# Hybrid SSD/S5 encoder block on one core: the down projection's quarter differences move to VectorE over three products, the SSD running sums' halves take another buffer, the group norm's sums are kept by step

## The chip, the core and the metric

One NeuronCore of a Trainium2 chip runs the whole kernel: TensorE (PE) multiplies, VectorE (DVE), ScalarE (ACT) and GpSimd (POOL) do everything else, SyncE (SP) issues most transfers, POOL and ACT a few. The metric is the device time of one execution in microseconds, the median of three runs; a profiled execution has its own time.

## What is computed

One layer of a residual encoder over 1024 tokens of width 1024, in float32:

```
h    = RMSNorm(x)
p    = h @ W_in                          # z | xBC | dt | u
y_A  = SSD (Mamba-2 chunked scan, both directions), gated by silu(z), RMS-normed in 2 groups of 512
y_B  = S5 scan, gelu, GLU
x    = x + RMSNorm(concat(y_A, y_B) @ W_out)
x    = x + RMSNorm((silu(h2 @ W_gate) * (h2 @ W_up)) @ W_down),   h2 = RMSNorm(x)
```

Two parts are touched by the change. In the SSD group the decays are exponentials of running sums over a chunk of 128 tokens, and the group norm divides by the root of the mean of y*y over the 512 channels of a group. The down projection is a product of 1024x2816 by 2816x1024.

## The kernel before

All matrix products are made from float32 split in a high half of reduced precision ("fp32r") and a low half, the rest; three matmuls (high by high, high by low, low by high) stand for one. A split is always the same pair: ScalarE copies the source to the high half, VectorE subtracts that from the source.

**The SSD stretch** (about 540 to 945 us). A scheduler, by priorities and a cost table of its own, merges two generators: the GLU of the S5 group (`glu`, matmuls recorded on L277, tiles `gh`, `glo`), then the output projection (`out_s5`, `out_g0`, matmuls L1169), and the eight SSD units (`unit(q)`, q = 0 to 7, each a pair of heads). `dt_prep` comes ahead of unit 0: it makes the running sums with `tri_le`/`tri_ge`, splits them into a tile `rhl` (high half by ScalarE on L890, low half by VectorE on L891), and writes these with eight transfers on POOL's queue to two DRAM tensors, `rr_d` (L894) and `na_d` (L895). `unit_loads` reads them back as `la` and `ra`, the two operands of the matmuls on L1013 whose exponentials are the decays. `rhl` sits in the buffer with the tag "X", of which there is one; unit 0's own `X` (tokens by channels, transposes on L903, copied by ScalarE on L904) has the same tag. From `X` come `Xw` (one half by VectorE, one by POOL, L975) and from that the chunk states (matmuls L988). At its end a unit squares y (L1064 or L1067), adds that to `ssum` (L1068), splits y into `hl` (L1072, L1073; tag "hl") and stores it on SP's queue (L1074, L1075). y lies token by token, token = 8k + l; `hl` is stored by step l, so L1072 reads y with a step of eight elements. `group_norm` sums `ssum` over channels with eight matmuls by a column of ones (L1082), whose stationary operand is a slice of `ssum` with a step of eight.

**The down projection** (about 1431 to 1668 us). It runs in the order of the program, as two levels of a seven-product scheme: the quarters of the activation (computed before, stored in `ff_d`) and of W_down are combined, and seven products P1, P2, P3, P6, P5, P7, P4, each over eleven slices q, give the four quarters of the result. One (product, slice) is twelve matmuls of 128x128 by 128x512 on L1898. `d_op(i)` prepares it: loads (`wd_load`, `da`), the two splits (ScalarE L1879, VectorE L1880), then `wd_sums`, which overwrites quarters of the weight tile `wd[q]` with differences that later products use. It runs five products ahead of the matmuls (`dla`); sixteen buffers with the tag "w8" hold the eleven `wd` tiles and five `dop` tiles, so at most four prepared products wait behind the one that runs. `DB` says which quarter a product uses: P3 the raw quarter 3, P6 the changed quarter 3, P5 quarter 0, P7 quarter 1, P4 quarter 2. `half_sum` squares a finished half row block on ScalarE and multiplies it by the norm's weight (L1933); `final` adds the residual (L1951).

Of the kernel before, what the change touches and what calls it, by code (L numbers as in the profile page):

```python
# [10 lines left out]
F32R = mybir.dt.float32r  # L11
I32 = mybir.dt.int32
AF = mybir.ActivationFunctionType
ALU = mybir.AluOpType
PSUM = bass.MemoryType.PSUM
ADD, SUB, MUL = ALU.add, ALU.subtract, ALU.mult
# [116 lines left out]
def hymba_block(ctx, tc, P, out, dbg=None, upto=99):  # L133
    nc = tc.nc

    @contextmanager
    def hpri(n):
        off = KN[n]
        if off:
            p = tc.cur_priority  # L140
            tc.cur_priority = p - off
        yield
        if off:
            tc.cur_priority = tc.cur_priority + off

    def pri(n):
        def deco(f):
            def g(*a, **k):
                with hpri(n):
                    return f(*a, **k)  # L150
            return g
        return deco

    act, dve, pool, pe, sp = nc.scalar, nc.vector, nc.gpsimd, nc.tensor, nc.sync
# [5 lines left out]
    def pd(k):  # L160
        return pool if k in KN['pd'] else dve
# [39 lines left out]
    def ptmp():  # L201
        return psB.tile([128, 512], F32, tag="tmp", name="ptmp")
# [112 lines left out]
    def rms_scale(ssum, rstd, inv_n, eps):  # L315
        dve.tensor_scalar(rstd, ssum, inv_n, eps, op0=MUL, op1=ADD)
        return pool.tensor_tensor(rstd, rstd, mhalf.to_broadcast(list(rstd.shape)), op=ALU.pow)
# [246 lines left out]
    HF = [slice(0, 512), slice(512, 1024)]  # L564
# [264 lines left out]
    def dt_prep():  # L829
# [54 lines left out]
        for d in range(2):  # L884
            pe.matmul(t[:, 128 * d:128 * d + 128], af[:, d].rearrange("p c h -> p (c h)"), (tri_le, tri_ge)[d], start=True, stop=True)
            pe.transpose(t[:, 256 + 128 * d:384 + 128 * d], ln[:, d].rearrange("p c h -> p (c h)"), ident)
        rhl = un.tile([128, 2, 4, 128], F32R, tag="X", name="rhl")
        rh, rl = rhl[:, 0], rhl[:, 1]
        tv = t.rearrange("p (n l) -> p n l", n=4)
        act.copy(rh, tv)  # L890
        dve.tensor_tensor(rl, tv, rh.bitcast(F32), op=SUB)  # L891
# [71 lines left out]
    def unit(q, ssum):  # L963
        g = q // 4
        with hpri("u1"):
# [4 lines left out]
            X = un.tile([128, 8, 128], F32, tag="X", name="X")  # L970
            transposes(X, xT)
            Xw = un.tile([128, 2, 8, 2, 64], F32, tag="Xw", name="Xw")
            for d in range(2):
                w = wdt[:, :, 16 * d + 2 * q:16 * d + 2 * q + 2].unsqueeze(3).to_broadcast([128, 8, 2, 64])
# [4 lines left out]
        with hpri("u2"):  # L979

            Sn = un.tile([128, 2, 7, 128], F32, tag="Sn", name="Sn")
            for s0 in range(0, 7, 2):
                t = ptmp()
                ns = min(2, 7 - s0)
                for d in range(2):
                    for s in range(ns):
                        c = s0 + s if d == 0 else 7 - s0 - s
                        pe.matmul(t[:, 256 * s + 128 * d:256 * s + 128 * d + 128], Bt[:, c, g, :],  # L988
                                  Xw[:, d, c].rearrange("p h e -> p (h e)"), start=True, stop=True)
                for s in range(ns):  # L990
# [4 lines left out]
                    for d in range(2):  # L995
                        for hh in range(2):
                            es = slice(64 * hh, 64 * hh + 64)
                            o = 256 * s + 128 * d + 64 * hh
# [4 lines left out]
        y = un.tile([128, 1024], F32, tag="yg", name="yg", bufs=2)  # L1003
        for hf in range(2):
# [21 lines left out]
            with hpri("u4"):  # L1026
# [10 lines left out]
                for j in range(4):  # L1037
                    c = 4 * hf + j
# [4 lines left out]
                for d in range(2):  # L1043
# [7 lines left out]
                    for j in range(j0, j1):  # L1051
                        c = 4 * hf + j
# [7 lines left out]
            if hf == 0:  # L1060
                yield
        with hpri("u4"):
            if q % 4 == 0:
                act.activation(ssum, y, AF.Square)  # L1064
            else:
                sq = io.tile([128, 1024], F32, tag="io", name="sq")
                act.activation(sq, y, AF.Square)  # L1067
                pd('ss').tensor_tensor(ssum, ssum, sq, op=ADD)  # L1068
            hl = un.tile([128, 2, 8, 128], F32R, tag="hl", name="hl")
            w = vec2[:, R_N + q:R_N + q + 1]  # L1070
            yv = y.rearrange("p (k l) -> p l k", l=8)
            act.activation(hl[:, 0], yv, AF.Copy, scale=w)  # L1072
            dve.scalar_tensor_tensor(hl[:, 1], yv, w, hl.bitcast(F32)[:, 0], op0=MUL, op1=SUB)  # L1073
            Q[KN["cq"]].dma_start(ch_d[128 * q:128 * q + 128], hl.bitcast(F32)[:, 0])  # L1074
            Q[KN["cq"]].dma_start(cl_d[128 * q:128 * q + 128], hl.bitcast(F32)[:, 1])  # L1075

    @pri("gn")
    def group_norm(g, ssum):
        t = ptmp()
        sv = ssum.rearrange("p (k l) -> p l k", l=8)  # L1080
        for l in range(8):
            pe.matmul(t[:, l:l + 1], sv[:, l, :], ones[:, 0:1], start=True, stop=True)  # L1082
        rms_scale(t[:, 0:8], rg[:, g, :], 1.0 / 512, 1e-5)
# [254 lines left out]
    with tc.manual_schedule():  # L1338
        next(cvs)
        pair_powers()  # L1340
        for n, blk in enumerate(blocks):
# [9 lines left out]
            b = n - NB + KC  # L1351
# [94 lines left out]
    un = ust.enter_context(tc.tile_pool(name="un", bufs=1))  # L1446
# [8 lines left out]
    def ssd():  # L1455
        for g in range(2):
            ssum = un.tile([128, 1024], F32, tag="ssum", name="ssum")
            for q in range(4 * g, 4 * g + 4):
                yield from unit(q, ssum)
                yield  # L1460
            group_norm(g, ssum)
            yield
# [16 lines left out]
    fill = glu()  # L1479
    next(fill)  # L1480
    dt_prep()
    fill_with(fill, 15, R_GLU)
    for _ in fill:
# [278 lines left out]
    for l in range(8):  # L1762
        b = MX["step"] * l
# [11 lines left out]
        for q in range(2):  # L1775
            at(b + MX["ev"] + 0.6 * q, turn_evac, l, q)
            if l < 4 or q:
                n = "12"[q] + "12"[l // 4]
# [44 lines left out]
    for i in range(14, len(prods)):  # L1823
        p, n, m = prods[i]
# [23 lines left out]
    def wd_load(n, q):  # L1848
        if n == "P1":
            wd.append(fp.tile([128, 4, 512], F32, tag="w8", name="wd", bufs=W_))  # L1850
            bl = ((0, 0, 0),)
        elif n == "P2":
            bl = ((2, 1, 0),)
        elif n == "P3":
            bl = ((3, 1, 1), (1, 0, 1))
        else:
            return
        for b, s_, c in bl:
            sp.dma_start(wd[q][:, b], wdv[s_, c][:, q])

    def wd_sums(n, q):
        w = wd[q]
        l = {"P3": ((0, 1, 0), (1, 3, 1), (3, 3, 0), (2, 2, 3))}.get(n, ())
        for o, a, b in l:
            pool.tensor_tensor(w[:, o], w[:, a], w[:, b], op=SUB)  # L1865

    def d_op(i):
        if i >= len(dprods) or i in dops:
            return
        n, q = dprods[i]  # L1870
        wd_load(n, q)
        if (n, q // 2) not in das:
            das[n, q // 2] = a = wst.tile([128, 2, 512], F32, tag=("whi", "wlo", "raw")[len(das) % 3], name="da", bufs=2)
            e = min(2, NP - q)
            sp.dma_start(a[:, 0:e], ff_d[int(n[1]) - 1, q:q + e].rearrange("q p k -> p q k"))
        a = das[n, q // 2][:, q % 2]
        dops[i] = t = fp.tile([128, 2, 2, 512], F32R, tag="w8", name="dop", bufs=W_)
        for k, src in enumerate((a, wd[q][:, DB[n]])):
            act.copy(t[:, k, 0], src)  # L1879
            dve.tensor_tensor(t[:, k, 1], src, t.bitcast(F32)[:, k, 0], op=SUB)  # L1880
        wd_sums(n, q)
# [5 lines left out]
    wp2 = fp.tile([128, 1024], F32, name="wp2")  # L1887
# [12 lines left out]
    def d_post(n, j, ps):  # L1900
        if n == "P1":
            act.copy(us[j], ps)
        elif n == "P2":
            dve.tensor_tensor(C11[j], us[j], ps, op=ADD)
            later.append((half_sum, j, 0))
        elif n == "P3":
            act.copy(C12[j], ps)
        elif n == "P6":
            dve.tensor_tensor(us[j], us[j], ps, op=ADD)
        elif n == "P5":  # L1910
            dve.tensor_tensor(ts_[j], us[j], ps, op=ADD)
            dve.tensor_tensor(C12[j], C12[j], ts_[j], op=ADD)
            later.append((half_sum, j, 1))
            if j == 3:
                later.extend([(final_load, 0), (final_load, 1), (final_scale, 0), (final, 0), (final_scale, 1), (final, 1), (final_store, 0), (final_load, 2), (final_store, 1), (final_load, 3),
                              (final_scale, 2), (final, 2), (final_scale, 3), (final, 3), (final_store, 2), (final_store, 3)])
        elif n == "P7":
            dve.tensor_tensor(C22[j], ts_[j], ps, op=ADD)
            dve.tensor_tensor(us[j], us[j], ps, op=ADD)
            later.append((half_sum, 4 + j, 1))  # L1920
            later.append((final_load, 4 + j))
        else:
            dve.tensor_tensor(C21[j], us[j], ps, op=ADD)
            half_sum(4 + j, 0)
            final(4 + j)

    def half_sum(l, c):
        f = fa[:, l, HF[c]]
        act.activation(jk2, f, AF.Square, accum_out=s5[:, c, l:l + 1])
        last = (l, c) in ((4, 0), (5, 0), (6, 0), (7, 0))  # L1930
        if last:
            final_scale(l)
        (dve if last else pool).tensor_tensor(f, f, wp2[:, HF[c]], op=MUL)  # L1933

    def final_scale(l):
        dve.tensor_tensor(s5[:, 2, l:l + 1], s5[:, 0, l:l + 1], s5[:, 1, l:l + 1], op=ADD)
        rms_scale(s5[:, 2, l:l + 1], s5[:, 3, l:l + 1], 1.0 / 1024, 1e-6)
# [73 lines left out]
```

## Time and profile before

| | us |
|---|---|
| median of 3 runs (lowest, highest) | 1672.16 (1668.52, 1672.4) |
| the profiled execution, its own time | 1669.68 |
| its span from first to last instruction | 1667.8 |
| PE busy in the span | 1546.0 (93%) |
| DVE busy | 1241.3 (74%) |
| ACT busy | 730.4 (44%) |
| POOL busy | 461.4 (28%) |

Starts of rows are microseconds from the span's start. The profiled execution's time is 1.9 us over its span and 2.5 us under the median. Busy shares are averages over stages with different limits; what an edit is worth is read from its own stage.

### The profile page before, as it was taken

To read this page: it belongs to the slowest core of one execution; us is meant where nothing else is said; L and a number is where in the kernel's file an instruction comes from. 1 tells how busy PE (TensorE), PEld (TensorE's weight loads), DVE (VectorE), ACT (ScalarE), POOL (GpSimd) and SP (SyncE) were. 2 spreads that over 40 slices of the span, in tenths; PEclk is the share of its full clock that TensorE was granted. 3 is DMA by queue.
4 is the path that set the end of the run, shared out by engine and by line. 5 is a ranking of instruction groups with operands and counts; after the bars stand their busy time and mean duration, and the time that the engine had idled before them with its cause. 6 is when DMAs were issued, how large, how long until landed. Compare 5 with 4: busy or idle time off the path is not lost.

```text
span 1667.8 us, 22199 instructions
## 1 busy us (share of the span) xinstructions
PE 1546.0 (93%) x7980; PEld 1263.7 (76%) x7980; DVE 1241.3 (74%) x1910; ACT 730.4 (44%) x1238; POOL 461.4 (28%) x455
## 2 busy tenths in 40 slices
PE   7999999999777889899999988999999999999897
PEld 6787788777775667778778766788888888787686
DVE  7549998888452687886666578788878887669777
ACT  6345632323887445444343476222223322344352
POOL 2110000000221120111110141555555544249412
PEclk9999999999898989999999998999999999999999
DMA  5553444433877657976588872332222221682234
GB/s 181 149 144 103 127 159 152 133 109 105 207 173 204 189 176 245 289 227 219 189 262 269 291 237 95 122 107 96 95 101 101 95 101 51 242 313 74 92 119 170
DMA packets 250000, 271.58 MB, mean 163 GB/s; under 512 B 29387, under 2 KB 190659, under 8 KB 249891
## 3 DMA queue, kind: packets, MB, share of 16 engines
q1 hardware_dynamic: 224515, 215.96, 41.6%
q0 software_dynamic: 12896, 33.83, 6.4%
q10 hardware_dynamic: 12480, 20.39, 3.4%
q8 instruction: 63, 1.03, 0.3%
q14 instruction: 46, 0.38, 0.1%
HBM read 185.23 MB, written 84.84 MB: 162 GB/s over the span
## 4 chain that ended last, share of the span: by engine, by line
PE 40%; DVE 10%; DMA 8%; issue 4%; ACT 4%; POOL 3%; SPq 0%; DVEq 0%; POOLq 0%; ACTq 0%
PE acc L1592 13%; PE ptmp L1592 10%; PE ptmp L1898 4%; PE acc L1169 3%; PE acc L1898 3%; DVE dop L1880 2%; PE acc L277 2%; DMA m<-m_d 2%; PE ptmp L988 1%; POOL wd L1865 1%; PE ptmp L1054 1%; DMA m_d<-m 1%; DMA oraw<-in_w_out_dram 1%; DVE cacc L756 1%; PE ptmp L1040 1%
## 5 line engine op out<-in xcount | busy, mean ns | idle before, releaser
L1169 PE MATMUL acc<-ohi,cat 128*128 128x512 f32 x512 | 173.3, 404 | 10.8 <-DMA cat<-ch_d 5.7
L277 PE MATMUL acc<-hTh,whi 128*128 128x512 f32 (+1 forms) x456 | 179.5, 394 | 0.4 <-ACT hTh L334 0.4
L277 PE MATMUL acc<-hTl,whi 128*128 128x512 f32 (+1 forms) x456 | 178.7, 392 | 0.5 <-DVE hTl L337 0.5
L277 PE MATMUL acc<-hTh,wlo 128*128 128x512 f32 (+1 forms) x456 | 178.0, 391 | 0.0
L1575 DVE TENSOR_TENSOR wop<-rawp,wop 128x512 fp32r<-128x512 f32 x120 | 137.7, 1148 | 17.9 <-ACT wop L1574 16.7
L1592 PE MATMUL ptmp<-T,wop 128*128 128x512 f32 x528 | 127.8, 398 | 4.1 <-ACT T L1748 3.7
L1592 PE MATMUL acc<-T,wop 128*128 128x512 f32 x528 | 125.7, 393 | 1.7 <-DVE T L1751 1.6
L1898 PE MATMUL ptmp<-dop 128*128 128x512 f32 x528 | 122.0, 392 | 2.9 <-DVE dop L1880 2.9
L1592 PE MATMUL acc<-B,wop 128*128 128x512 f32 x528 | 124.6, 391 | 0.0
L1169 PEld LDWEIGHTS acc<-ohi,cat 128*128 128x128 f32 x512 | 97.7, 192 | 34.4 <-DVE mix L1720 5.4
L1592 PEld LDWEIGHTS ptmp<-T,wop 128*128 128x128 f32 x528 | 101.0, 192 | 27.3 <-ACT T L1748 3.9
L1898 PEld LDWEIGHTS ptmp<-dop 128*128 128x128 f32 x528 | 100.1, 190 | 24.2 <-DVE dop L1880 3.2
L1592 PEld LDWEIGHTS acc<-T,wop 128*128 128x128 f32 x528 | 98.8, 188 | 25.1 <-DVE T L1751 3.4
L1592 PEld LDWEIGHTS acc<-B,wop 128*128 128x128 f32 x528 | 99.0, 188 | 21.9 <-DVE B L1751 0.3
L1607 ACT ACTIVATE cg<-cg 128x512 f32<-128x512 f32 x44 | 27.8, 633 | 183.0 <-DVE cg L1605 183.0
L1574 ACT CAST wop<-rawp 128x512 fp32r<-128x512 f32 x120 | 70.2, 615 | 76.7 <-POOL rawp L1549 51.2
L1880 DVE TENSOR_TENSOR dop<-da,dop 128x512 fp32r<-128x512 f32 x77 | 75.1, 975 | 37.5 <-ACT dop L1879 37.4
L1898 PE MATMUL acc<-dop 128*128 128x512 f32 x396 | 95.6, 398 | 7.4 <-DVE dop L1880 4.7
L1169 PE MATMUL acc<-olo,cat 128*128 128x512 f32 x256 | 101.9, 398 | 0.4 <-DVE olo L1133 0.4
L277 PEld LDWEIGHTS acc<-hTh,whi 128*128 128x128 f32 x456 | 86.7, 190 | 19.4 <-issue 1.7
L277 PEld LDWEIGHTS acc<-hTl,whi 128*128 128x128 f32 x456 | 86.7, 190 | 18.4 <-DVE hTl L337 1.0
L277 PEld LDWEIGHTS acc<-hTh,wlo 128*128 128x128 f32 x456 | 86.7, 190 | 17.1 <-DVE wlo L268 0.2
(368 smaller groups left out, 3400.5 us busy)
## 6 DMA issues: line engine op xcount, KB each, us to landing
ff_d<-cg POOLq DMA_DIRECT2D x77, 256.0 KB, 2.3
da<-ff_d SPq DMA_DIRECT2D x35, 512.0 KB
raw<-in_w_in_dram SPq DMA_DIRECT2D x28, 512.0 KB
cat<-ch_d SPq DMA_DIRECT2D x48, 256.0 KB
cat<-cl_d SPq DMA_DIRECT2D x48, 256.0 KB
wd<-in_w_down_dram SPq DMA_DIRECT2D x44, 256.0 KB
rawp<-in_w_gate_dram SPq DMA_DIRECT2D x10, 1024.0 KB
rawp<-in_w_up_dram SPq DMA_DIRECT2D x10, 1024.0 KB
```

What stands on the lines that cost most here:

```text
L277: pe.matmul(ps, a[:, k, :], b[:, k, sl], start=(k == 0 and n == 0), stop=(k == 7 and n == 2))
L756: (pool if ct in KN['pc'] and k in KN['pk'] else dve).scalar_tensor_tensor(a[:, d], xp[:, r], w[k], a[:, d], op0=MUL, op1=ADD)
L988: pe.matmul(t[:, 256 * s + 128 * d:256 * s + 128 * d + 128], Bt[:, c, g, :], Xw[:, d, c].rearrange("p h e -> p (h e)"), start=True, stop=True)
L1040: pe.matmul(yd[64 * hh:64 * hh + 64, 128 * j:128 * j + 128], X[:, c, 64 * hh:64 * hh + 64], Ms[hh][:, j, :], start=True, stop=True)
L1054: pe.matmul(yo[:, 128 * j:128 * j + 128], Sn[:, d, st, :], CT[:, g, 128 * c:128 * c + 128], start=True, stop=True)
L1169: pe.matmul(ps, c[:, a, k % 4, :], b[:, k % 2, :], start=(k == 0 and n == 0), stop=(k == n_ - 1 and n == 2))
L1574: act.copy(t[:, 0], src)
L1575: dve.tensor_tensor(t[:, 1], src, t.bitcast(F32)[:, 0], op=SUB)
L1592: pe.matmul(ps, a[:, ai, k, :], b[:, bi, k, :], start=(k == 0 and q == 0), stop=(k == 3 and q == 2))
L1607: act.activation(cg[:, 0], cg[:, 0], AF.Silu)
L1880: dve.tensor_tensor(t[:, k, 1], src, t.bitcast(F32)[:, k, 0], op=SUB)
L1898: pe.matmul(ps, t[:, 0, a, 128 * j:128 * j + 128], t[:, 1, b, :], start=(q == 0 and n == 0), stop=(q == NP - 1 and n == 2))
```

## The change

Four edits. `rhl` takes the tag "hl" in place of "X" (it fills half of that tile). The squares of y are written by step: L1064 and L1067 now read y with a step of eight and write in order, and `group_norm` reads `ssum` in order. In the down projection quarter 1 of the weights is loaded with P2 in place of P3; of the four differences one is made with P2, two with P3 and one with P6, where all four were made with P3, and they go from POOL to VectorE. The multiplications by the norm's weight that POOL made go to VectorE too.

```diff
-        rhl = un.tile([128, 2, 4, 128], F32R, tag="X", name="rhl")
-        rh, rl = rhl[:, 0], rhl[:, 1]
+        rhl = un.tile([128, 2, 8, 128], F32R, tag="hl", name="rhl")
+        rh, rl = rhl[:, 0, 0:4], rhl[:, 1, 0:4]
...
+            yv = y.rearrange("p (k l) -> p l k", l=8)
             if q % 4 == 0:
-                act.activation(ssum, y, AF.Square)
+                act.activation(ssum.rearrange("p (l k) -> p l k", l=8), yv, AF.Square)
             else:
                 sq = io.tile([128, 1024], F32, tag="io", name="sq")
-                act.activation(sq, y, AF.Square)
+                act.activation(sq.rearrange("p (l k) -> p l k", l=8), yv, AF.Square)
                 pd('ss').tensor_tensor(ssum, ssum, sq, op=ADD)
...
-        sv = ssum.rearrange("p (k l) -> p l k", l=8)
+        sv = ssum.rearrange("p (l k) -> p l k", l=8)
...
         elif n == "P2":
-            bl = ((2, 1, 0),)
+            bl = ((2, 1, 0), (1, 0, 1))
         elif n == "P3":
-            bl = ((3, 1, 1), (1, 0, 1))
+            bl = ((3, 1, 1),)
...
-        l = {"P3": ((0, 1, 0), (1, 3, 1), (3, 3, 0), (2, 2, 3))}.get(n, ())
+        l = {"P2": ((0, 1, 0),), "P3": ((1, 3, 1), (3, 3, 0)), "P6": ((2, 2, 3),)}.get(n, ())
         for o, a, b in l:
-            pool.tensor_tensor(w[:, o], w[:, a], w[:, b], op=SUB)
+            dve.tensor_tensor(w[:, o], w[:, a], w[:, b], op=SUB)
...
-        (dve if last else pool).tensor_tensor(f, f, wp2[:, HF[c]], op=MUL)
+        dve.tensor_tensor(f, f, wp2[:, HF[c]], op=MUL)
```

The order in the down projection is the program's. Here is VectorE around the end of P2, before: the pairs of splits, and P2's four sums (L1904).

```order
L1880 TENSOR_TENSOR dop<-da,dop 128x512
L1880 TENSOR_TENSOR dop<-wd,dop 128x512
L1904 TENSOR_TENSOR fa<-fa,acc 128x512 x4
L1880 TENSOR_TENSOR dop<-da,dop 128x512
L1880 TENSOR_TENSOR dop<-wd,dop 128x512
```

And the same place after (lines from 1064 on have moved by one):

```order
L1881 TENSOR_TENSOR dop<-da,dop 128x512
L1881 TENSOR_TENSOR dop<-wd,dop 128x512
L1866 TENSOR_TENSOR wd<-wd 128x512 x2
L1905 TENSOR_TENSOR fa<-fa,acc 128x512 x4
L1881 TENSOR_TENSOR dop<-da,dop 128x512
L1881 TENSOR_TENSOR dop<-wd,dop 128x512
L1866 TENSOR_TENSOR wd<-wd 128x512 x2
L1934 TENSOR_TENSOR fa<-fa,wp_11882 128x512
```

Each pair of splits of P3 is now followed by two differences (L1866), and the first four also by a multiplication (L1934).

In the SSD stretch the scheduler places the rows anew, on every engine from the running sums of `dt_prep` on; PE's order is the old one again from the last blocks of the GLU on. On POOL, at the writes of `rhl`, the difference is:

```order
 L940 MEMSET efs 128x256
 L894 DMA rr_d<-rhl 8x16x128
+L975 TENSOR_TENSOR Xw<-X,wdt 128x1024
 L895 DMA na_d<-rhl 2x64x128
 L894 DMA rr_d<-rhl 8x16x128
@@ -99,5 +100,4 @@
 L894 DMA rr_d<-rhl 8x16x128
 L895 DMA na_d<-rhl 2x64x128
-L975 TENSOR_TENSOR Xw<-X,wdt 128x1024
 L1034 TENSOR_TENSOR M<-E 128x512
```

Unit 0's `Xw` on POOL stood behind all eight writes and now stands behind the first, so seven writes are issued after it. On PE, before, 44 matmuls of the GLU stand between the last transpose of `dt_prep` (L886) and unit 0's chunk states (L988), one between these and the decays' matmuls (L1013, L1014):

```order
L277 MATMUL acc<-gh,whi 128x512
L277 MATMUL acc<-glo,whi 128x512
L988 MATMUL ptmp<-Xw,Bt 128x128 x14
L277 MATMUL acc<-gh,wlo 128x512
L1013 MATMUL ptmp<-ra_4786,la_4785 128x512
L1014 MATMUL ptmp<-neg,idr 128x512
```

After, 18 stand ahead of the chunk states and 22 between these and the decays' matmuls (four of the 44 have gone ahead of the transposes); here is the first of the two places:

```order
L277 MATMUL acc<-gh,wlo 128x512
L277 MATMUL acc<-gh,whi 128x512
L988 MATMUL ptmp<-Xw,Bt 128x128 x14
L277 MATMUL acc<-glo,whi 128x512
L277 MATMUL acc<-gh,wlo 128x512
```

Some two dozen matmuls of the GLU have moved from ahead of the chunk states to behind them.

## Rows read from the trace of the kernel before

**Rows 1.** Busy time by stretch: window, us, PE, PEld, DVE, ACT, POOL, PEclk, DMA share, GB/s

```profile
1431.00:1490.00 59.00, 56.11 (x242) 46.38 (x242) 36.04 (x49) 27.29 (x51) 10.99 (x11) 0.97 0.94 345
1490.00:1530.00 40.00, 39.38 (x173) 31.98 (x172) 39.67 (x28) 21.40 (x42) 38.67 (x24) 1.00 0.28 89
1530.00:1566.00 36.00, 29.19 (x111) 20.62 (x110) 31.00 (x23) 9.49 (x18) 31.98 (x21) 0.96 0.20 67
```

**Rows 2.** PE in order of time, blocks P3, P6 and P5: start, us

```profile
1495.06 30.08 PE L1898 MATMUL ptmp<-dop 128*128 128x512 f32 x132
1524.97 0.39 PE L1898 MATMUL acc<-dop 128*128 128x512 f32 x1
...
1567.64 30.11 PE L1898 MATMUL ptmp<-dop 128*128 128x512 f32 x132
```

**Rows 3.** POOL in order of time, its differences in the down projection

```profile
1486.47 36.82 POOL L1865 TENSOR_TENSOR wd<-wd 128x512 f32<-128x512 f32 x22 [11.49 <-DVE dop L1880]
...
1550.43 12.57 POOL L1865 TENSOR_TENSOR wd<-wd 128x512 f32<-128x512 f32 x8
```

**Rows 4.** DVE in order of time, splits beside POOL and after POOL has ended

```profile
1508.47 1.78 DVE L1880 TENSOR_TENSOR dop<-da,dop 128x512 fp32r<-128x512 f32 x1
...
1564.07 0.68 DVE L1880 TENSOR_TENSOR dop<-wd,dop 128x512 fp32r<-128x512 f32 x1
1564.67 0.68 DVE L1880 TENSOR_TENSOR dop<-da,dop 128x512 fp32r<-128x512 f32 x1
```

**Rows 5.** ACT in order of time, a split of P6; idle time before it in brackets

```profile
1547.10 0.62 ACT L1879 CAST dop<-wd 128x512 fp32r<-128x512 f32 x1 [7.35 <-POOL wd L1865]
```

**Rows 6.** A group from 1220 us on: count, busy us, mean ns, idle before

```profile
L1865 POOL TENSOR_TENSOR wd<-wd 128x512 f32<-128x512 f32 x44 | 70.5, 1606 | 49.4 <-DMA wd<-in_w_down_dram 35.4 <-DVE dop L1880 11.5
```

**Rows 7.** The chain of waits in the tail: start, us, what

```profile
1641.14 3.40 DVE fa L1951 x2
...
1645.00 5.43 DMA xr<-x_d
...
1650.52 1.42 DVE fa L1951 x2
```

**Rows 8.** POOL in order of time, in the tail

```profile
1640.92 6.03 POOL L1933 TENSOR_TENSOR fa<-fa,wp 128x512 f32<-128x512 f32 x4
```

**Rows 9.** PE in order of time, unit 0's chunk states

```profile
587.08 1.19 PE L988 MATMUL ptmp<-Xw,Bt 128*128 128x128 f32 x4 [9.14 <-DVE Xw L975]
588.75 5.37 PE L988 MATMUL ptmp<-Xw,Bt 128*128 128x128 f32 x24 [0.48 <-POOL Xw L975]
```

**Rows 10.** The chain of waits, the last write of rhl and Xw

```profile
575.56 8.97 DMA na_d<-rhl
...
585.75 2.95 POOL Xw L975
```

**Rows 11.** Busy time by stretch, columns as in rows 1, unit 0's chunk states

```profile
587.00:594.00 7.00, 6.44 (x29) 6.17 (x30) 6.43 (x17) 2.14 (x4) 1.70 (x1) 0.51 0.41 116
```

**Rows 12.** ACT's groups of 128x1024 from 128x1024, columns as in rows 6

```profile
L1072 ACT ACTIVATE hl<-yg,vec 128x1024 fp32r<-128x1024 f32 x8 | 18.4, 2303 | 0.0
...
L1729 ACT ACTIVATE xn<-xr,s 128x1024 f32<-128x1024 f32 x8 | 9.2, 1152 | 6.5 <-POOL s L1716 6.5
...
L1067 ACT ACTIVATE sq<-yg 128x1024 f32<-128x1024 f32 x6 | 6.4, 1059 | 22.3 <-DVE yg L1059 22.3
```

**Rows 13.** The chain of waits at the ends of units 2 and 7

```profile
724.99 1.06 ACT sq L1067
...
914.50 2.38 ACT hl L1072
...
919.55 4.28 DMA m<-m_d
```

**Rows 14.** PE in order of time, group 0's norm sums and a stretch of chunk states

```profile
764.05 3.26 PE L1082 MATMUL ptmp<-ones,ssum 128*128 128x1 f32 x14
...
680.80 1.83 PE L988 MATMUL ptmp<-Xw,Bt 128*128 128x128 f32 x14 [0.99 <-POOL Xw L975]
```

More of the change, by code (lines that the diff above doesn't have):

```diff
@@ L1070, in unit @@
             w = vec2[:, R_N + q:R_N + q + 1]
-            yv = y.rearrange("p (k l) -> p l k", l=8)
             act.activation(hl[:, 0], yv, AF.Copy, scale=w)
```

## The prediction

> **What bounds the kernel now.** Over the span TensorE is the busy engine, so the question is where it waits. I read the table of busy time by stretch first. In the down projection PE fills the stretch to 1530, but VectorE and POOL fill it too, 39.67 and 38.67 of 40 us; in the next 36 us PE is busy for 29.19 only, while the DMA queues lie at a share of 0.20 [rows 1]. So it is an engine that holds PE there, no transfer.
>
> PE's own timeline shows how much that is. Product P3 takes from 1495.06 to 1524.97, that is 29.91 us for 132 matmuls, without a wait. P6, the same 132 matmuls, takes from 1524.97 to 1567.64, that is 42.67 [rows 2]. **The loss is 42.67 - 29.91 = 12.76 us**, and no other product has one of its kind.
>
> The cause is read on three engines. POOL makes the weight differences without a break from 1486.47 to 1563.0 [rows 3], 44 of them at 1606 ns [rows 6], with the multiplications between. While it does, a split on VectorE takes 1.78 us; as soon as POOL is through, the same instruction takes 0.68 and the next one starts 0.60 later [rows 4]. Two splits at 1.7 us apart are 3.4 us a product where PE needs 29.91 / 11 = 2.72, so VectorE falls behind through P3 and eats the four prepared products. In P6 ScalarE waits as well, 7.35 us at once, for a quarter that POOL has not made yet [rows 5]. Both waits have one source: POOL does this work at 1.6 us an instruction and makes VectorE slow meanwhile.
>
> **The change part by part.**
>
> *Differences and multiplications to VectorE.* POOL loses all 44 differences and its 12 multiplications (16 halves less the last four); it keeps only the small power of the norm. With POOL idle I take 0.68 us for each of these on VectorE, at a spacing of 0.60 [rows 4]: same shape, same two operands in SBUF. (From above: 1.78, if something else than POOL should make these slow; then see the rivals.) A product of P2 or P6 needs two splits and one difference, 3 x 0.60 = 1.8 us of PE's 2.72. P3 needs two splits and two differences, 4 x 0.60 = 2.4 a product, 26.4 for eleven, and beside that P2's four sums and four multiplications, 8 x 0.60 = 4.8: together 31.2 us against PE's 29.91. VectorE falls back by 1.3 us; with single durations of 0.68 instead of the spacing (52 x 0.68 = 35.4) by 5.5 us. The cover is the four prepared products, 4 x 2.72 = 10.9 us, which are full when P3 begins, as P2 leaves VectorE a third of its time. So PE should not wait in P3 or P6. P6's quarter 3 is then made with P3, eleven products ahead of its use. **Term: -12.7 us** (bounds: 0 and -12.8).
>
> *Quarter 1 with P2.* Eleven loads of 256 KB come eleven products earlier. In the stretch where they fall the DMA engines move 345 GB/s at a share of 0.94 [rows 1]; P2's product then needs 3 x 0.262 MB (two quarters of weights, one of activations) in 2.72 us, 289 GB/s, and P3's needs 193 where it needed 289. Less than the rate shown, so hidden behind P1 and P2's matmuls. Were the cover gone, 11 x 0.262 MB at 345 GB/s would be 8.4 us. I take 0.
>
> *The tail.* With P4's matmuls four multiplications on POOL (6.03 us in all [rows 8]) run beside the last residual of the first four row blocks, which takes 3.40 us for two instructions; undisturbed, two such take 1.42 [rows 7]. The store of that block and the loads of the last four `xr` are queued behind it on SP: they start at 1645.00 and land at 1650.4, and the final work of block 4 on VectorE waits for that [rows 7]. With POOL idle the loads start 3.40 - 1.42 = 2.0 us earlier. Against that VectorE now makes the four multiplications itself, 4 x 0.60 = 2.4 us, directly behind that residual, in a place where it would wait for the loads anyway. What follows per block is serial on VectorE and goes along. **Term: -1.8 us** (0 to -2.0).
>
> *`rhl` in another buffer.* Now unit 0's X waits for the last write of `rhl`, which lands at 575.56 + 8.97 = 584.53 [rows 10], and PE waits 9.14 us for the `Xw` made of it [rows 9]. After, X is copied at once. But two things give most of that back. First, on POOL's queue `Xw` (2.95 us [rows 10]) now stands behind the first write, so the other seven are issued later by that, and ScalarE makes the two copies of X ahead of the running sums: the last write lands near 588. Second, `la` and `ra` are read back from these writes, and the decays' matmuls need them: a load on SP's queue lands some 4 us after its issue (4.28 in [rows 13]), so they can start near 592. Before, they started one matmul behind the chunk states, whose rows end at 588.75 + 5.37 = 594.1 [rows 9]. So the wait moves from the chunk states to the decays and PE gains about 2 us of its 9.14. The clock takes part of it: behind the wait the granted clock was 0.51, the lower of the two levels (1.2 GHz against 2.4), and 24 matmuls took 5.37 us, 0.224 each [rows 9, 11], where elsewhere 14 take 1.83, 0.131 each [rows 14]. With a wait ahead of the decays, their ten larger matmuls pay instead. **Term: -1.2 us** (+1 to -9.1, the whole wait).
>
> *Squares by step.* Eight squares on ScalarE, 1059 ns each now. What they will cost is shown by a neighbour: the same engine's copy of the same y with the step of eight takes 2303 ns, while a copy with a scale that reads in order takes 1152 [rows 12]. I take 2.3 us, 1.25 more each, 10.0 for eight (bounds: 0 and 10). Of that counts what lies on the path: unit 2's square and unit 7's stand in the chain of waits, and behind unit 7's the split and then the load of `m` on SP's queue [rows 13]; of the other six I count one. **Term: +3.7 us.**
>
> The Trainium skill speaks against this edit ("SBUF — State Buffer", section "Door 1: The DMA port swizzle"): SBUF is read in lines of 16 bytes, and each access that passes to a new line pays. A step of eight float32 passes to a new line with every element. By it all eight squares become slow, and the sum would be the same as by the row of the copy; the column sums below would become faster, for the same reason.
>
> *`ssum` read in order.* Fourteen loads and matmuls by the column of ones took 3.26 us, 0.233 each [rows 14]; a stationary operand of the same size read in order gives 0.131 a matmul [rows 14]. Sixteen for a group are 1.6 us, of which group 0's lie in a stretch that PE fills; group 1's lie ahead of a wait for `m` and gain nothing. **Term: -1.4 us.**
>
> **Sum:** -12.7 - 1.8 - 1.2 + 3.7 - 1.4 = -13.4 us on an execution of 1669.68, that is 1656.3. The median shown lies 2.5 us above that execution, the lowest run 1.2 below; I give 1657.
>
> **The rivals.**
>
> *A. VectorE becomes the bound.* In P3 it has 52 instructions (44 + 8). PE waits as soon as they take more than 29.91 + 10.9 = 40.8 us, 0.785 each; the whole gain of P6 is used up at (40.8 + 12.8) / 52 = 1.03 us each, and at 1.7, today's spacing, the down projection would be about 35 us slower, some 1692. For it: 1.7 us is what rows of this very stretch show. Against it: the splits fall back to 0.68 in the moment POOL ends [rows 4], with the same operands, and POOL has nothing left to do.
>
> *B. The SSD stretch eats the gain.* All eight slow squares lie on the path (+10.0) and the decays wait as long as the chunk states did (no gain from `rhl`): -12.7 - 1.8 + 10.0 = -4.5, 1665. For it: the units' work feeds loads on SP's in-order queue. Against it: between the first and the last unit PE is the engine that ends most pieces of the chain.
>
> *C. The wait for `rhl` goes entirely*, and PE's clock with it: -9.1 in place of -1.2, 1648 to 1649. Against it: the decays still need data that leave later.
>
> *D. The loads with P2 come late:* up to 8.4 us of the gain, 1665. Against it: the rate above.
>
> **How the numbers follow.** Forecast, P6's wait gone and the SSD stretch within a few us either way: 0.66, its own range 1652 to 1662. C 0.13, B 0.10, D 0.04, A with a gain left 0.02 and A slower 0.05. What a measurement of this kernel can tell from no change is 0.3%, 5 us. Forecast, C, and the better halves of B, D and A are faster by more: 0.87; within 0.3%: 0.08; slower: 0.05. The range reaches to C's 1648 and to B's and D's 1666.
>
> **What would show it.** Right: PE without waits from P1's second product to P4's end, each product 29.9 us; splits at 0.68 to 0.69 throughout; no POOL rows of 128x512 in the down projection; squares at 2.3 us; PE's wait ahead of L988 short and a new one ahead of L1013. Wrong: splits above 0.79 in P3, waits in P6 for quarter 3, ScalarE waiting for `wd` in P2, or a stretch from 600 to 945 that is longer by 10 us.

## The result, and the profile after

The changed kernel took 1655.13 us (median of 4 runs, 1652.01 to 1658.1), the kernel before beside it 1670.34 (1666.61 to 1672.4): ratio 0.990, 95% interval 0.9868 to 0.9931. Forecast were 1657 and 1648 to 1666. The profiled execution took 1653.32 us, its span is 1651.6 where it was 1667.8. A second comparison on another chip, told below, gave 0.994 (0.9914 to 0.9966), so the two comparisons put the gain at 15 and at 10 us.

The table of busy time by stretch, changed kernel, same windows and columns as [rows 1]:

```profile
1431.00:1490.00 59.00, 58.10 (x250) 47.97 (x251) 41.77 (x65) 27.71 (x50) 2.82 (x4) 0.97 0.96 351
1490.00:1530.00 40.00, 40.00 (x178) 33.14 (x177) 37.76 (x62) 21.58 (x42) 0.00 (x0) 1.00 0.30 97
1530.00:1566.00 36.00, 36.00 (x161) 29.80 (x160) 22.78 (x37) 14.85 (x26) 0.00 (x0) 1.00 0.30 99
```

PE is busy in all of the last two stretches, where [rows 1] show 29.19 of 36 us for the last, and POOL has nothing left to do in them. PE in order of time (start, us), from P1's second row on, against [rows 2]:

```profile
1431.90 31.48 PE L1899 MATMUL ptmp<-dop 128*128 128x512 f32 x131 [2.88 <-DVE dop L1881]
1463.22 30.08 PE L1899 MATMUL acc<-dop 128*128 128x512 f32 x132
1493.14 30.08 PE L1899 MATMUL ptmp<-dop 128*128 128x512 f32 x132
1523.06 30.08 PE L1899 MATMUL acc<-dop 128*128 128x512 f32 x132
1552.98 30.08 PE L1899 MATMUL ptmp<-dop 128*128 128x512 f32 x132
```

P3 (at 1493.14) and P6 (at 1523.06) now take 29.92 us each, without a wait inside. VectorE's groups between 1463 and 1530 (count, busy us, mean ns, idle before) answer to [rows 4, 6]:

```profile
L1866 DVE TENSOR_TENSOR wd<-wd 128x512 f32<-128x512 f32 x36 | 24.7, 686 | 0.4
L1881 DVE TENSOR_TENSOR dop<-wd,dop 128x512 fp32r<-128x512 f32 x26 | 17.8, 685 | 0.0
L1881 DVE TENSOR_TENSOR dop<-da,dop 128x512 fp32r<-128x512 f32 x25 | 17.2, 689 | 8.3 <-ACT dop L1880 7.8
```

All three kinds take 0.69 us. VectorE still waits 8.3 us, mostly for ScalarE's copies to `dop` (which themselves wait for PE to free the buffers, 30.4 us in this stretch), so it is not the bound. The tail's chain of waits, against [rows 7]:

```profile
1626.45 1.34 DVE fa L1952 x2
1627.80 0.34 SPq L1957
1628.14 0.05 issue
1628.23 6.01 DMA xr<-x_d
1634.34 1.42 DVE fa L1952 x2
```

The residual took 3.40 us and takes 1.34; the load in the chain starts 1628.23 - 1612.82 = 15.4 us behind P4's start, where it started 1645.00 - 1627.51 = 17.5 behind it. ScalarE's squares, in groups, against [rows 12]:

```profile
L1069 ACT ACTIVATE sq<-yg 128x1024 f32<-128x1024 f32 x6 | 12.9, 2147 | 22.2 <-DVE yg L1059 22.2
L1066 ACT ACTIVATE ssum<-yg 128x1024 f32<-128x1024 f32 x2 | 4.2, 2110 | 8.7 <-DVE yg L1059 8.7
```

And PE around unit 0's chunk states and decays, against [rows 9]:

```profile
573.68 4.99 PE L988 MATMUL ptmp<-Xw,Bt 128*128 128x128 f32 x28 [2.68 <-DVE Xw L975]
...
584.77 0.47 PE L1013 MATMUL ptmp<-ra,la 128*128 128x512 f32 x1 [1.04 <-DVE wlo L268]
```

Counted from the start of VectorE's `ln` (L880, which runs ahead of every edited line; at 561.55 here and at 563.45 before), the chunk states start after 12.1 us instead of 23.6, and the decays' first matmul after 23.2 instead of 30.7. How much of such a lead arrives at the end is a question for more than one execution.

### Stages of all profiled executions

Starts wander before any edited line has run: `ln` starts between 560.35 (e6) and 573.59 (e5) in these executions, and in the two of the changed kernel at 561.55 and 568.90 (e8). So two spans, or two starts, can't simply be compared. From rows of each profile I took five lengths. A: from `ln` (one instruction) to PE's first decay matmul (L1013). B: from `ln` to the first matmul of the output projection (L1169, L1170 after). C: from `ln` to P1's first matmul, the whole SSD stretch and the MLP's first half. D: from there to the end of P4's last matmul. E: from there to the span's end. Before, for instance, D is 1627.51 + 30.08 - 1430.66 = 226.9.

| kernel | A | B | C | D | E |
|---|---|---|---|---|---|
| before | 30.7 | 120.2 | 867.2 | 226.9 | 10.2 |
| changed | 23.2 | 119.3 | 867.1 | 214.3 | 8.7 |
| e1_down_only | 29.1 | 119.5 | 867.6 | 214.3 | 8.6 |
| e2_hl_only | 23.2 | 119.6 | 869.1 | 227.3 | 9.8 |
| e3_squares_only | 29.4 | 120.7 | 871.7 | 228.6 | 9.9 |
| e4_dve_with_p3 | 29.0 | 120.0 | 865.9 | 224.3 | 8.4 |
| e5_pool_spread | 23.3 | 121.8 | 874.2 | 220.0 | 9.1 |
| e6_mul_on_pool | 23.2 | 119.5 | 872.2 | 212.8 | 10.5 |
| e7_no_squares | 23.5 | 117.0 | 864.0 | 214.2 | 9.1 |
| e8_changed_again | 23.6 | 119.6 | 868.9 | 214.5 | 8.3 |
| e9_square_behind | 22.9 | 122.3 | 872.3 | 212.8 | 7.6 |
| e10_inorder_behind | 23.6 | 120.1 | 873.5 | 214.4 | 7.9 |
| e11_ghl_on_pool | 23.1 | 118.4 | 867.2 | 215.6 | 11.1 |
| e12_step_group0 | 23.2 | 122.9 | 869.2 | 212.8 | 8.6 |

### The profile page after: what moved, and what is told of

Read it like the earlier page. It is cut to its first block, busy times and chain, and to the rows that moved or that the text cites. A ratio compares the mean times of both kernels' runs of the same rounds, so it can differ in the third digit from the quotient of the medians.

```text
span 1651.6 us, 22158 instructions
## 1 busy us (share of the span) xinstructions
PE 1538.8 (93%) x7980; PEld 1261.8 (76%) x7980; DVE 1226.8 (74%) x1966; ACT 738.3 (45%) x1238; POOL 371.9 (23%) x399
## 4 chain that ended last, share of the span: by engine, by line
PE 45%; DVE 9%; DMA 6%; issue 3%; ACT 3%; POOL 1%; SPq 0%; DVEq 0%; POOLq 0%; ACTq 0%
PE acc L1593 13%; PE ptmp L1593 10%; PE ptmp L1899 6%; PE acc L1899 5%; PE acc L1170 4%; PE acc L277 3%; DMA m<-m_d 1%; PE ptmp L1054 1%; PE ptmp L988 1%; DMA m_d<-m 1%; DVE cacc L756 1%; DVE dop L1881 1%; DMA cl_d<-ghl 1%; PE ptmp L1040 1%; DMA cat<-ch_d 1%
## 5 line engine op out<-in xcount | busy, mean ns | idle before, releaser
L1170 PE MATMUL acc<-ohi,cat 128*128 128x512 f32 x512 | 173.7, 404 | 12.3 <-DMA cat<-ch_d 6.5
L1170 PEld LDWEIGHTS acc<-ohi,cat 128*128 128x128 f32 x512 | 97.8, 192 | 35.9 <-DVE m L1199 6.9
L1170 PE MATMUL acc<-olo,cat 128*128 128x512 f32 x256 | 101.9, 398 | 0.3 <-DVE olo L1134 0.3
L1880 ACT CAST dop<-da 128x512 fp32r<-128x512 f32 x77 | 48.0, 623 | 97.9 <-PE acc L1899 38.6
L1614 POOL TENSOR_TENSOR cg<-cg 128x512 f32<-128x512 f32 x44 | 61.9, 1407 | 130.1 <-DVE cg L1609 129.5
```

The costliest lines, as they stand in the source:

```text
L1170: pe.matmul(ps, c[:, a, k % 4, :], b[:, k % 2, :], start=(k == 0 and n == 0), stop=(k == n_ - 1 and n == 2))
L1614: pool.tensor_tensor(dst, a, b, op=op)
```

## The experiments

Ratios are to the kernel before on the same chip: 1675.1 us for the first four, 1674.92 for the next four, 1673.36 for the last four (medians of 26 runs each).

### e1: the down projection alone

The kernel before with the change's edits of the down projection; the differences and multiplications are on VectorE. (In the cuts of code from here on, `...` stands for lines left out.)

```diff
-bl = ((2, 1, 0),)
+bl = ((2, 1, 0), (1, 0, 1))
...
-bl = ((3, 1, 1), (1, 0, 1))
+bl = ((3, 1, 1),)
...
-l = {"P3": ((0, 1, 0), (1, 3, 1), (3, 3, 0), (2, 2, 3))}.get(n, ())
+l = {"P2": ((0, 1, 0),), "P3": ((1, 3, 1), (3, 3, 0)), "P6": ((2, 2, 3),)}.get(n, ())
...
-pool.tensor_tensor(w[:, o], w[:, a], w[:, b], op=SUB)
+dve.tensor_tensor(w[:, o], w[:, a], w[:, b], op=SUB)
...
-(dve if last else pool).tensor_tensor(f, f, wp2[:, HF[c]], op=MUL)
+dve.tensor_tensor(f, f, wp2[:, HF[c]], op=MUL)
```

> The kernel before with the edits of the down projection alone: differences and multiplications on VectorE, spread over P2, P3 and P6, quarter 1 loaded with P2. Forecast: P6's wait (12.7 us) and 1.8 us of the tail go, nothing else: 14.5 us less, a ratio of 0.991; product blocks of 29.9 us from P1 to P4, splits at 0.68. Rival (part of the gain comes from the SSD stretch): less than 10 us here, ratio above 0.994.

Measured 1660.83 us, ratio 0.9901 (0.988 to 0.9923); D 214.3, E 8.6. The edits of the down projection alone reach the changed kernel's ratio (0.990 and, in e8, 0.994).

### e4 and e5: engine and place apart

e4 takes VectorE for the differences and multiplications, but leaves all four differences beside P3 and quarter 1's load with P3. e5 spreads them, but on POOL; it differs from the changed kernel in the engine of the differences alone.

```diff
 # e4: before, and
-pool.tensor_tensor(w[:, o], w[:, a], w[:, b], op=SUB)
+dve.tensor_tensor(w[:, o], w[:, a], w[:, b], op=SUB)
...
-(dve if last else pool).tensor_tensor(f, f, wp2[:, HF[c]], op=MUL)
+dve.tensor_tensor(f, f, wp2[:, HF[c]], op=MUL)
 # e5: changed, and
-dve.tensor_tensor(w[:, o], w[:, a], w[:, b], op=SUB)
+pool.tensor_tensor(w[:, o], w[:, a], w[:, b], op=SUB)
```

> The kernel before with the 44 differences and all multiplications on VectorE, but all four differences of a quarter beside P3 and quarter 1 loaded with P3, as before. If the engine alone made the loss, all of P6's 12.7 us and the tail's 1.8 go: ratio 0.991. By the count of the prediction VectorE then has 66 + 8 instructions in P3, at 0.60 us 44.4 us against 29.9 of PE and 10.9 of cover: waits of 3.6 us, at 0.68 us 9.5: ratio 0.993 to 0.997, with P3's own block at 33 to 39 us. If the place of the differences was the cause and not POOL, P6 waits as before: ratio 1.0.

> The changed kernel with the 44 differences on POOL again, but spread over P2, P3 and P6 as the change has them; the multiplications stay on VectorE. If POOL's work beside VectorE is the cause, splits are at 1.7 us wherever POOL works (17.6 us of P2, 35.2 in P3): P3 then needs 30 instructions of VectorE at 1.7, 51 us against 29.9 and 10.9 of cover, so PE waits about 10 us in P3 and the start of P6, and most of the 12.7 us is lost again: ratio to before 0.994 to 0.999. If spreading and the earlier load of quarter 1 were what counts, PE has no wait and the ratio is that of the changed kernel, 0.987 to 0.990.

Measured: e4 1668.34 us, 0.9967 (0.994 to 0.9995); e5 1671.77, 0.9962 (0.9933 to 0.9991). PE in e4, P3 from 1498.21 and P6 from 1536.85:

```profile
1498.21 16.73 PE L1898 MATMUL ptmp<-dop 128*128 128x512 f32 x73
1516.44 3.02 PE L1898 MATMUL ptmp<-dop 128*128 128x512 f32 x12 [1.50 <-DVE dop L1880]
...
1536.85 0.39 PE L1898 MATMUL acc<-dop 128*128 128x512 f32 x1
...
1568.00 30.08 PE L1898 MATMUL ptmp<-dop 128*128 128x512 f32 x132
```

and VectorE in e4, one product of P3:

```profile
1515.10 0.68 DVE L1880 TENSOR_TENSOR dop<-da,dop 128x512 fp32r<-128x512 f32 x1
1515.70 0.69 DVE L1880 TENSOR_TENSOR dop<-wd,dop 128x512 fp32r<-128x512 f32 x1
1516.30 2.86 DVE L1865 TENSOR_TENSOR wd<-wd 128x512 f32<-128x512 f32 x4
1519.08 0.68 DVE L1933 TENSOR_TENSOR fa<-fa,wp 128x512 f32<-128x512 f32 x1
1519.68 0.69 DVE L1880 TENSOR_TENSOR dop<-da,dop 128x512 fp32r<-128x512 f32 x1
```

In e5, VectorE in the first third of P6 (1544.26 to 1577.83), and POOL there:

```profile
1547.88 1.78 DVE L1881 TENSOR_TENSOR dop<-da,dop 128x512 fp32r<-128x512 f32 x1
1549.59 1.78 DVE L1881 TENSOR_TENSOR dop<-wd,dop 128x512 fp32r<-128x512 f32 x1
```

```profile
1542.39 20.32 POOL L1866 TENSOR_TENSOR wd<-wd 128x512 f32<-128x512 f32 x12
```

and VectorE's sums and multiplications of e5 from 1500 to 1535, in groups:

```profile
L1934 DVE TENSOR_TENSOR fa<-fa,wp 128x512 f32<-128x512 f32 x4 | 2.7, 680 | 0.0
L1905 DVE TENSOR_TENSOR fa<-fa,acc 128x512 f32<-128x512 f32 x4 | 2.5, 675 | 0.0
```

P3 and P6 together should take 59.84 us. They took 72.6 before (12.7 over), 1568.00 - 1498.21 = 69.8 in e4 (10.0 over), 1577.83 - 1513.54 = 64.29 in e5 (4.45 over), and 59.84 as changed. So VectorE alone wins 2.7 of the 12.7 us, spreading alone 8.3, and only both together all. The two ratios cannot be told apart; these lengths can. Two things might blur them. e5 has the multiplications on VectorE, but e6 (below) has them on POOL, and its P3 and P6 take 29.92 us each. And spreading includes the earlier load of quarter 1, which P2's difference reads; but in e4, where it comes with P3, neither VectorE nor ScalarE waits for a load between 1498 and 1540.

In e4 no split is slow (0.69 us), and still PE waits 1.5 us a product: VectorE has seven instructions for one (two splits, four differences, one multiplication), 1519.68 - 1515.10 = 4.58 us against PE's 2.72. My count for that place, 74 instructions at 0.68 against 40.8 us, gave 9.5; it was 10.0. My figure for e5, 10, was too high: it took all 30 of VectorE's instructions in P3 as slow. Splits beside POOL were, at 1.78 us, but the eight sums and multiplications took 0.68 (the sums, which read PSUM, beside a busy POOL; the multiplications, which began in pauses of POOL). That is 8 us less and leaves 2; of the 4.45 measured, 0.8 fall in P3 and 3.65 in P6, where PE advances by 3.4 us a product while POOL still works.

### e6: the multiplications on POOL again

```diff
 # changed, and
-dve.tensor_tensor(f, f, wp2[:, HF[c]], op=MUL)
+(dve if last else pool).tensor_tensor(f, f, wp2[:, HF[c]], op=MUL)
```

> The changed kernel with the 12 multiplications on POOL again. Forecast: the tail's 1.8 us come back, with the residual of the first four row blocks at 1.7 us an instruction and the last loads later; in P3 four multiplications slow VectorE for 6 us, which the prepared products cover. 1.8 us slower than the changed kernel. Rival (the tail's term is not real, the end hangs on the last product alone): no difference, and the same distance from P4's start to the end. Rival (POOL's four in P3 tip VectorE over): a wait in P3, 3 us or more.

Measured 1664.21 us, 0.992 (0.989 to 0.995), not to be told from the changed kernel beside it (e8, 1664.92). The tail's chain shows the mechanism all the same:

```profile
1628.87 3.40 DVE fa L1952 x2
...
1632.73 5.69 DMA xr<-x_d
```

The residual is at 3.40 us again and the load starts 17.5 us behind P4's start (1615.22). The other profiles agree: 17.49 to 17.51 us with the multiplications on POOL (before, e2, e3, e6), 15.41 to 15.43 in the ten others. E spreads more, 9.8 to 10.5 in the four (mean 10.1) and 7.6 to 11.1 in the ten (mean 8.7): the load itself takes 5.0 to 6.4 us, and in e11 the span ends 5.6 us behind the issue of the last store where it is 3.1 in the changed kernel.

### e2 and e3: the buffer alone, the squares alone

```diff
 # e2: before, and
-rhl = un.tile([128, 2, 4, 128], F32R, tag="X", name="rhl")
-rh, rl = rhl[:, 0], rhl[:, 1]
+rhl = un.tile([128, 2, 8, 128], F32R, tag="hl", name="rhl")
+rh, rl = rhl[:, 0, 0:4], rhl[:, 1, 0:4]
 # e3: before, and (the same for ssum)
-act.activation(sq, y, AF.Square)
+act.activation(sq.rearrange("p (l k) -> p l k", l=8), yv, AF.Square)
...
-sv = ssum.rearrange("p (k l) -> p l k", l=8)
+sv = ssum.rearrange("p (l k) -> p l k", l=8)
```

> The kernel before with rhl in the buffer of the running sums' halves alone. Forecast: PE's wait ahead of the chunk states goes and a wait ahead of the decays takes its place, 1.2 us less, which no five rounds show: ratio 0.998 to 1.001. Rival C (the whole wait is won): 9.1 us less, ratio 0.9945. Third way, suggested by the trace of the changed kernel: the decays come 7 to 8 us earlier too, and the gate's matmuls behind them wait in their place until the lead is used up, by 660 us or so: net within 1 us of nothing.

> The kernel before with the squares written by step and the column sums read in order, nothing else. Forecast: +3.7 - 1.4 = 2.3 us more, ratio 1.001; squares at 2.1 us where they took 1.06, column sums at 0.13 us a matmul. Rival B (all eight on the path): 8 us more, ratio 1.005. Rival (all hidden): 1.4 us less, 0.999.

Measured: e2 1668.8 us, 0.996 (0.994 to 0.998); e3 1676.45, 1.0004 (0.9984 to 1.0024). e2's profiled execution shows the third way: A is 6 to 7 us shorter, B as ever. It was one of the longer executions of e2, though (1676.28), and the 6 us of the median are not seen in it. By its ratio e2 misses its forecast (0.998 to 1.001), and its interval holds rival C's 0.9945. But its 12 executions also had a higher granted clock on average, 0.9728 where the 26 of the kernel before had 0.9698; by the two halves of e2 told at the end (0.9758 and 0.9697, 8 us apart) that is about 4 of the 6 us, an estimate. Whether the edit itself raises that clock is not shown.

### e7 and e8: the changed kernel without the squares' edit, and itself

```diff
 # e7: changed, and (the same for ssum)
-act.activation(sq.rearrange("p (l k) -> p l k", l=8), yv, AF.Square)
+act.activation(sq, y, AF.Square)
...
-sv = ssum.rearrange("p (l k) -> p l k", l=8)
+sv = ssum.rearrange("p (k l) -> p l k", l=8)
```

> The changed kernel with squares in order and column sums by step, as before; everything else as changed. Forecast: 2.3 us faster than the changed kernel (3.7 of the squares less 1.4 of the sums). With half of it hidden, as the run of that edit alone suggests: 0 to 1.5 us. Rival B: 8 us faster.

> The changed kernel itself, on this chip beside its variants. If the parts add up (0.990 for the down projection alone, 0.996 for the buffer alone, 1.000 for the squares alone), ratio 0.986, 23 us less than before. If the lead that the buffer wins is given back in the stretch behind it, and only the down projection counts: 0.990.

Measured: e7 1660.18 us, 0.9901 (0.9866 to 0.9936); e8 1664.92, 0.994 (0.9914 to 0.9966). The parts do not add up to the 23 us; e7 is as fast as e1. Its median is the lower one, but its interval and e8's overlap.

### e12, e9 and e10: where the squares count

e12 leaves the squares of group 1 in order. e9 puts each square and its sum behind the copy, split and stores of `hl`; e10 does that with squares in order.

```diff
 # e12: changed, and for g == 1 (the same for ssum and its column sums)
-act.activation(sq.rearrange("p (l k) -> p l k", l=8), yv, AF.Square)
+act.activation(sq, y, AF.Square)
...
 # e9: changed, moved
-if q % 4 == 0:
...
 Q[KN["cq"]].dma_start(cl_d[128 * q:128 * q + 128], hl.bitcast(F32)[:, 1])
+if q % 4 == 0:
...
```

> The changed kernel with the squares of group 1 (units 4 to 7) in order again, those of group 0 by step as changed; the order of instructions is the changed kernel's. If unit 7's square on the path makes the cost: the stretch from 880 to 960 loses the 1.5 to 3.4 us that it gained in the runs with the squares by step, and the time is that with all squares in order or a little less (column sums of group 0 in order): ratio 0.989 to 0.990. If group 0's squares cost as much: half of that, 0.992.

> The changed kernel with each unit's square and its sum behind the copies and splits of hl and their stores, instead of ahead of them. If the slow squares cost because unit 7's copy of hl, its split and the load of m on SP's queue stand behind the square, then unit 7's copy starts when y is ready, about 2 us sooner, the stretch 840 to 1000 is 2 to 3.5 us shorter than the changed kernel's, and the ratio to before is 0.991. If the squares are hidden anyway or cost elsewhere (column sums, ScalarE's load): the changed kernel's time, 0.994.

> The changed kernel with squares in order (as before) and, besides, behind the copies of hl. Unit 7's copy of hl then waits for no square at all: 1 us less than with the squares in order ahead of it, so 0.989 to 0.990, if that path ends last; no difference to the changed kernel with squares in order (0.990) if it doesn't.

Measured: e12 1660.74 us, 0.9925 (0.9896 to 0.9954); e9 1660.25, 0.9923 (0.9894 to 0.9951); e10 1662.92, 0.9938 (0.991 to 0.9966). By their ratios none differs from e8 (0.994) by more than the intervals allow, so the times decide nothing here; e10's expectation, 0.989 to 0.990 in either case, was missed. In their stages, from the start of unit 7's last gate multiplication (L1059) to unit 7's copy of `hl`, it is 1.74 us with squares in order ahead, 2.7 to 2.9 by step, 0.77 with the square behind; but C of e9 and e10 is no shorter (872.3 and 873.5): from `ln` to that multiplication it is 354.8 and 356.1 us where e8 has 349.5, more than what was won behind it. So the 1.1 us on unit 7's path are shown, and where the rest of the squares' cost lies is not.

### e11: the gate's stores on POOL's queue

```diff
 # changed, and
- 'hq': 's',
+ 'hq': 'g',
```

> The changed kernel with the stores of the gate's halves (ghl) issued on POOL's queue instead of SP's. In the profile of the changed kernel the decays come 9 to 10 us earlier and that lead is gone by 640, while SP waits 27.2 us for ghl in the stretch 570 to 690 where it waited 18.3 before, with the gate's weight loads queued behind. If that queue gives the lead back, some of it stays here: 2 to 6 us faster than the changed kernel, ratio 0.990 to 0.992. If the lead is lost to something else (the transfers themselves, ScalarE's order, the clock): no change, or slower by POOL's issue times, 0.994 to 0.997.

Measured 1666.36 us, 0.9963 (0.9934 to 0.9992): no gain. B is 118.4 and C 867.2, at the low end of the by-step runs, and nothing of that arrives in the time (E is 11.1 in this execution).

## Why the prediction was right, and where it was not

**P6's wait: right, and the cause was two things.** Forecast -12.7; P6 fell from 42.67 to 29.92 us. D is 227.6 on average with the differences on POOL beside P3 (before, e2, e3) and 214.0 in the changed form (e1, e6, e7, e8, changed): -13.6. The two kernels' own profiles differ by 226.9 - 214.3 = 12.6; the rest of the mean is P1, whose length varies from execution to execution (D is 212.8 in e6). But the prediction put the loss on POOL alone ("both waits have one source"). e4 and e5 show that the place counts for more: VectorE undisturbed would still be late beside P3. The count by which the change was costed, so many instructions at 0.60 to 0.69 against PE's 29.91 and the cover of four products, held for the changed form and for e4.

**Quarter 1 with P2: right.** The DMA engines ran at a share of 0.96 and 351 GB/s in the stretch of the loads, and PE waits nowhere in P2 or P3. Rival D falls, and rival A with the 0.69 us. (Rival A's price was wrong by its own count: 52 x 1.7 - 40.8 = 47.6 us of waiting in place of 12.8 is 34.8 on top of 1669.7, some 1704; the 1692 adds it to a time from which the 12.7 had gone already.)

**The tail: right.** The load starts 2.1 us earlier behind P4's start in every profile with the multiplications on VectorE, where 2.0 were forecast. E fell by 10.1 - 8.7 = 1.4 us where 1.8 were; the load's own time varies by more than the difference.

**`rhl`: the size near, the working wrong.** The step that failed is that the last write lands near 588 and the decays can start only near 592, that is 24.6 and 28.6 us behind `ln`. DMA writes of `na_d` in the changed kernel, from its rows (issue to landing):

```profile
L895 POOL DMA_DIRECT2D na_d<-rhl x4: 801/801/852, 572.4 to 576.6; - x4
...
DMA to landing us min/median/max: 3.7/4.9/5.8
```

The last is issued 576.6 - 561.55 = 15.0 us behind `ln`, where it was 575.56 - 563.45 = 12.1 before: 2.9 us later, as forecast (1.0 for the two copies of X, 1.92 for `Xw` on POOL). But it lands at most 5.8 us after its issue, not 9, and the decays start at 23.2. Why the writes land sooner was not tried. So the decays come about 6 us earlier in every run with the other buffer (A: 22.9 to 23.6 against 29.0 to 30.7). That lead is gone by the output projection: B is 119.5 to 120.7 without the buffer's edit and 117.0 to 122.9 with it. Where it goes is seen between the decays' first matmul and the output projection's, first before, then in the changed kernel (columns as in [rows 1]):

```profile
594.19:683.66 89.47, 81.29 (x436) 63.78 (x434) 70.67 (x110) 45.47 (x67) 12.45 (x8) 1.00 0.74 239
584.77:680.84 96.07, 85.63 (x437) 68.47 (x437) 71.90 (x103) 50.30 (x73) 14.89 (x8) 0.95 0.75 237
```

PE is idle for 10.4 us instead of 8.2, and its busy time for the same work is 85.6 instead of 81.3, with the granted clock at 0.95 instead of 1.00. The other profiles agree: idle 8.0 to 8.6 us, busy 81.3 to 83.0 and clock 0.98 to 1.00 in the four with the old buffer, 10.1 to 11.8, 83.4 to 88.7 and 0.92 to 0.98 in the ten with the new one. On average 2.9 us of the lead go to more waiting and 3.4 to matmuls that take longer. Four of the waits in the changed kernel:

```profile
601.39 0.40 PE L1040 MATMUL ptmp<-M,X 128*64 128x128 f32 x2 [2.75 <-DVE M L1035]
...
615.97 0.50 PE L277 MATMUL acc<-glo,whi 128*128 128x512 f32 x1 [1.30 <-DVE glo L1104]
...
624.17 0.50 PE L277 MATMUL acc<-gh,whi 128*128 128x512 f32 x1 [1.52 <-ACT whi L267]
...
626.51 0.79 PE L277 MATMUL acc<-gh,wlo 128*128 128x512 f32 x1 [0.94 <-DVE wlo L268]
627.10 0.63 PE L277 MATMUL acc<-gh,whi 128*128 128x512 f32 x1
```

Those four are 6.5 us, and behind the last a matmul takes 0.63 us instead of 0.39: the granted clock averages 0.79 from 624 to 632, so for part of that stretch it was the lower of its two levels (1.2 GHz against 2.4). So the wait moved, and part of it turned into slower matmuls, as forecast; but it moved to the gate's operands and `M` behind the decays, not to the decays, ahead of which PE waits 1.04 us. In C the buffer's edit makes 866.6 (e2, e7) of 866.9 (before, e1, e4): -0.3, with 5 us between e2 and e7. Rival C, the whole 9.1 us, is not seen in C; e2's median of -6 us is not repeated by e7 against e1 or by e8, and what the clock does not account for stays unexplained. That the gate's stores on SP give the lead back was argued from SP's waits and is not borne out by e11's time.

**Squares: right in direction, the size not settled.** Each takes 2.1 us where 2.3 were forecast from the copy; 1.08 more each. C is 866.8 with squares in order (before, e1, e2, e4, e7; 864.0 to 869.1) and 870.8 by step (changed, e3, e5, e6, e8; 867.1 to 874.2): +4.0 where the two terms gave 3.7 - 1.4 = +2.3. With e9 and e11 (872.3 and 867.2, by step) and e10 (873.5, in order) it is +2.6, though e9 and e10 also move the squares; so that the term was too small is not shown. Rival B's 10 us are excluded by e3. The column sums did become cheaper (14 in 1.62 us, [rows 14] have 3.26), but that they shorten anything is not shown. For the squares the Trainium skill ("SBUF — State Buffer", section "Door 1: The DMA port swizzle") had named the direction; the size came from the row of the copy. The measured 2.1 agrees with both.

**The sum.** From the stages: -13.6 - 1.4 - 0.3 + 4.0 = -11.3 us (-12.7 with +2.6 for the squares), where -13.4 were forecast. Measured were 1670.34 - 1655.13 = -15.2 on the first chip and 1664.92 - 1674.92 = -10.0 on the second. That the first came within 2 us of 1657 is partly luck. Of the 16.2 us between its two profiled spans 12.6 are D, 1.5 are E and 0.1 are C; 1.9 lie ahead of `ln`, where nothing was edited, and e8's profiled execution of the same kernel reached `ln` 7.4 us later. It also lost nothing in C (867.1), while e3, e5, e6 and e8 lost 2 to 7.

## What to carry to other kernels

Count, for each stage, the instructions of the helping engine against the time of the engine that it feeds and the operands prepared ahead; moving work to a faster engine won little here where its place stayed overfull (2.7 of 12.7 us), and spreading it won more (8.3). A wait that was removed in the middle of a stretch paced by other loads and engines was handed on here: look for the lead again one stage later before it is entered in the sum. Read a stride's cost from the same engine's strided instruction on the same tile.

## What was not expected of the hardware

Of e2's 12 executions the six with a mean granted clock of 0.974 or more took 1662.24 to 1667.6 us (mean 1665.5), the six with 0.973 or less 1669.99 to 1677.66 (mean 1673.8): one program, and 8 us between its halves, more than any single edit of the SSD stretch. Why the clock differs between executions was not tried. And unit 0's pair of multiplications that make `Xw`, one on VectorE and one on POOL, started within 0.3 us of each other, took 1.23 and 2.94 us before, 3.29 and 1.92 in the changed kernel: either of the two engines can be the slow one. What decides it was not tried.
